# Delta-rule layer: the triangular inverse's small products spread behind projection products, its two 64-row blocks side by side

## The chip, the cores and the metric

The kernel runs on one core of a Trainium2 chip (trn2). The metric is the device time of one execution in microseconds (us), the median of several runs. In the text PE is TensorE (matrix products; PEld its weight loads), DVE is VectorE, ACT is ScalarE, POOL is GpSimd and SP is SyncE, which issues the DMAs here.

## The reference

The kernel computes one inference step of a two-layer decoder trunk for a prompt of 1024 tokens and 64 sample tokens (8 sequences of 8). Layer 0 mixes by a gated delta rule, layer 1 by dilated window attention. The change touches layer 0 alone. There each of 8 heads projects keys, queries and values, runs them through a causal convolution of width 4, and then, in chunks of tokens, solves a unit lower triangular system whose matrix comes from the keys:

```python
proj = jnp.einsum('bld,de->ble', h, w_in)
qkv, new_buf = causal_conv_silu(qkv, conv_buf, conv_w)
kb = kc * bc[..., None]
n_mat = jnp.where(strict, jnp.einsum('nbhik,nbhjk->nbhij', kb, kc) * decay, 0.0)
a_mat = n_mat + jnp.eye(C, dtype=n_mat.dtype)
rhs = jnp.concatenate([vc * bc[..., None], kb * jnp.exp(gc)[..., None]], axis=-1)
sol = lax.linalg.triangular_solve(a_mat, rhs, left_side=True, lower=True, unit_diagonal=True)
...
S, o = lax.scan(step, S0, (w_val, k_cum, qk, q_dec, k_dec, g_tot))
```

The scan then carries the state S from chunk to chunk. The reference uses chunks of 64 tokens; the kernel takes 128 tokens a chunk, 8 chunks of the prompt (the sample tokens are a ninth part with a path of their own), and forms the inverse of the triangular matrix of each chunk explicitly.

## The kernel before

Everything of layer 0 is done head by head, in stages that are emitted one after the other. `stage_k(h)` makes the keys: `conv_tile` loads a 1024x128 weight tile, splits it into a high and a low part, and `project` (line 128) runs 72 products for three column blocks of 384, 384 and 320 tokens (8 slices of the contraction by 3 combinations of high and low parts, 24 products a block), each into a bank called pp. These are the projection products. Each block then passes through the convolution on ACT, DVE and GpSimd (tiles xin and ca, line 72). After that come transposes (line 600), the products of keys with keys (line 655, into ps), the system matrix MT, and small products for the sample tokens (lines 664 to 691).

The inverse of a 128x128 triangular matrix is built up from its diagonal blocks of 32 rows. The 32x32 blocks of MT go to DRAM and back (line 696 writes msc, line 699 reads Mi), so that all 32 blocks of a head lie one on a partition, four times over; a substitution chain of 62 instructions on DVE (lines 710 and 712: a product into vtmp, a sum into Vi, once per row) inverts them; line 714 writes the result vsc and line 719 reads it into Vt, now as diagonal blocks of 8 matrices of 128x128. `stage_qv(h)` makes queries and values in the same way as the keys.

`stage_inverse(h)` completes Vt. Line 766 transposes the eight matrices (eight products 128x128, copied by ACT at line 767 into VT). Then, for the two 64-row blocks one after the other (p0 of 0 and 64): eight products 32x32 of MT and VT (line 773), an ACT copy into Aw (line 774), eight products 32x32 of Aw and Vt (line 777), and a DVE copy into Vt (line 778). The last step joins the two 64-row halves: eight transposes 64x64 (line 782) and a copy (783), eight products 64x64 (line 786) and a copy (787), eight products (line 790) and the DVE copy of line 791. Then `keys_by_token` uses Vt (lines 809 and 810), and DVE turns the result into vn (line 812). All these products write banks of one pool called lv, which has two buffers (`sbank`).

`stage_scan(h)` is the chain over the chunks: products at lines 896, 899, 907 and 910 (bank sc), with DVE steps between them (line 72, tiles w, S and o), `finish` (lines 828 to 835: a norm, a transpose at 832, a copy, a store), and between the hops the small products of the sample tokens, `sample()` (lines 850, 861, 867 and 877).

The emission order is keys 0, queries and values 0, keys 1, inverse 0; then for each head h: scan h, queries and values h+1, keys h+2, inverse h+1; the output gate's products stand with heads 6 and 7. The engines run their own instructions strictly in order. This order isn't the emitted one: a scheduler of the framework, with its own estimate of durations, sorts each engine's instructions, and `order_after` adds an edge that only orders two instructions of one engine. `newest[0]` holds the last product of the latest projection block.

Instructions on fp32 operands show as two passes in the trace (a count of x16 for eight products); the order listing counts products once.

## Time and profile before

| | |
|---|---|
| median of three runs | 2446.84 us (2445.88 to 2450.79) |
| the profiled execution | 2428.75 us, of which its span is 2427.0 us |
| PE busy | 2282.0 us, 94% of the span |
| DVE busy | 1376.6 us, 57% |
| ACT busy | 941.6 us, 39% |
| POOL busy | 260.4 us, 11% |
| chain that ended last | PE 67%, DMA 13%, DVE 9%, issue 6% |

The profiled execution is one run; its span is the time from the first to the last instruction of the trace. Busy time of PE counts a product until its modelled end, so that a busy PE can still be one that runs products slowly. The granted clock is the share of full speed that PE was given in a stretch; 0.50 is half speed.

### The profile page before, as it was taken

How to read it: one execution, taken by the hardware profiler on the slowest of the kernel's cores; microseconds unless marked ns; L12 is line 12 of the kernel's file. 1: busy time of each engine (PE TensorE's matmuls, PEld its weight loads, DVE VectorE, ACT ScalarE, POOL GpSimd, SP SyncE). 2: the span in 40 equal slices, each digit the busy share in tenths (PEclk: the TensorE clock that was granted, in tenths of full speed). 3: DMA queues.
4: the chain of work that ended last, by engine and by line, in shares of the span. 5: the costliest groups of instructions: out<-in, count | busy, mean ns of one | idle time of the engine just before them, and what ended most of it. 6: DMA issues, size and time to landing. Idle time of an engine off the chain costs nothing.

```text
span 2427.0 us, 43290 instructions
## 1 busy us (share of the span) xinstructions
PE 2282.0 (94%) x16647; PEld 2147.1 (88%) x16647; DVE 1376.6 (57%) x3414; ACT 941.6 (39%) x2477; POOL 260.4 (11%) x418
## 2 busy tenths in 40 slices
PE   7799999999999999899999999899998999999997
PEld 5688788779889898799988999899998999999897
DVE  6678767866875437327643374633737337375334
ACT  6445444444544324333233432334323333225234
POOL 3213222222321102200000000000000000000000
PEclk9889889888989999799999999999999999999999
DMA  9223223233223355439732497744967349785634
GB/s 324 62 68 91 63 74 84 60 73 79 79 77 97 88 158 165 131 84 335 228 109 74 132 345 204 237 115 125 351 197 249 115 122 340 198 288 169 213 103 148
DMA packets 482255, 379.42 MB, mean 156 GB/s; under 512 B 46206, under 2 KB 457071, under 8 KB 482048
## 3 DMA queue, kind: packets, MB, share of 16 engines
q1 hardware_dynamic: 482048, 376.65, 51.4%
q8 instruction: 131, 2.15, 0.4%
q14 instruction: 76, 0.62, 0.1%
HBM read 322.31 MB, written 54.27 MB: 155 GB/s over the span
## 4 chain that ended last, share of the span: by engine, by line
PE 67%; DMA 13%; DVE 9%; issue 6%; ACT 3%; POOL 1%; SPq 1%; POOLq 0%; ACTq 0%; DVEq 0%
PE pp L128 46%; DMA DT<-gcscr 2%; PE ps L1182 2%; PE ps L1200 2%; DMA qb<-qscr 2%; PE sc L1400 2%; DVE pr L1351 1%; DMA kc<-in_cache_kv_w_dram 1%; DMA wraw<-in_a_w_in_dram 1%; PE ps L1146 1%; DMA out_kv_s_dram<-knew 1%; PE ps L1191 1%; DMA aw<-in_ada_w_dram 1%; PE ps L150 1%; DMA out_y_p_dram<-yn 1%
## 5 line engine op out<-in xcount | busy, mean ns | idle before, releaser
L128 PE MATMUL pp<-hh,whi 128*128 128x384 f32 (+1 forms) x2688 | 915.2, 341 | 12.2 <-DVE vT L1140 4.2
L128 PE MATMUL pp<-hl,whi 128*128 128x384 f32 (+1 forms) x2688 | 906.1, 337 | 1.3 <-POOL hl L211 1.3
L128 PE MATMUL pp<-hh,wlo 128*128 128x384 f32 (+1 forms) x2688 | 901.5, 336 | 1.2 <-DVE wlo L111 1.2
L128 PEld LDWEIGHTS pp<-hh,whi 128*128 128x128 f32 x2688 | 514.0, 191 | 25.5 <-DVE vT L1140 6.6
L128 PEld LDWEIGHTS pp<-hl,whi 128*128 128x128 f32 x2688 | 514.6, 191 | 9.1 <-issue 4.6
L128 PEld LDWEIGHTS pp<-hh,wlo 128*128 128x128 f32 x2688 | 512.9, 191 | 6.3 <-issue 2.7
L111 DVE TENSOR_TENSOR wlo<-wraw,whi 128x1024 fp32r<-128x1024 f32 x136 | 170.2, 1251 | 127.7 <-ACT whi L110 126.9
L110 ACT CAST whi<-wraw 128x1024 fp32r<-128x1024 f32 x144 | 150.6, 1046 | 235.2 <-PE pp L128 146.2
L1187 ACT ACTIVATE sm<-sm,stg 128x128 f32<-128x128 f32 (+1 forms) x192 | 86.6, 451 | 359.8 <-DVE stg L1185 317.5
L1351 DVE TENSOR_TENSOR pr<-kc,qb 128x1024 f32<-128x1024 f32 x128 | 154.9, 1219 | 89.9 <-DMA qb<-qscr 56.2
L1341 DVE TENSOR_REDUCE ST<-pr 128x8 f32<-128x1024 f32 x128 | 153.7, 1214 | 1.1
L435 POOL TENSOR_TENSOR ol<-zo,oh 128x384 fp32r<-128x384 f32 x9 | 9.2, 1017 | 1302.6 <-ACT oh L434 1285.7
L72 DVE SCALAR_TENSOR_TENSOR ca<-xin,cwT,ca 128x384 f32<-128x384 f32 (+1 forms) x216 | 130.4, 608 | 7.6 <-ACT ca L577 6.2
L1185 DVE CUSTOM_DVE_ANT_0 sm<-ps,mA 128x256 f32<-128x256 f32 (+1 forms) x128 | 48.3, 377 | 137.1 <-PE ps L1182 136.2
L1200 PE MATMUL ps<-vnat,pT 128*128 128x128 f32 x560 | 96.3, 279 | 4.4 <-DVE pT L1196 4.4
L710 DVE TENSOR_TENSOR vtmp<-Vi,Mi 128x2 f32<-128x2 f32 (+30 forms) x248 | 95.7, 386 | 4.4 <-PE ps L690 0.7
L1182 PE MATMUL ps<-kT,qT 128*128 128x128 f32 (+1 forms) x384 | 93.3, 324 | 3.8 <-DVE stg L1185 3.6
L1200 PEld LDWEIGHTS ps<-vnat,pT 128*128 128x128 f32 x560 | 85.6, 189 | 10.6 <-ACT pTn L1380 4.2
L1194 ACT COPY pT<-ps 128x256 f32<-128x256 f32 (+1 forms) x96 | 32.4, 337 | 114.7 <-PE ps L1191 113.5
L128 PE MATMUL pp<-oh,whi 128*128 128x384 f32 (+1 forms) x216 | 72.0, 333 | 2.7 <-DVE zt L72 2.7
L72 DVE SCALAR_TENSOR_TENSOR hh<-pp,GT,xr 128x384 f32<-128x384 f32 (+1 forms) x48 | 27.3, 571 | 83.0 <-PE pp L128 79.2
L1185 DVE CUSTOM_DVE_ANT_0 sm<-ps,mG 128x128 f32<-128x128 f32 x64 | 18.4, 288 | 98.6 <-PE ps L1182 69.1
(449 smaller groups left out, 3681.5 us busy)
## 6 DMA issues: line engine op xcount, KB each, us to landing
qb<-qscr SPq DMA_DIRECT2D x128, 512.0 KB
kc<-in_cache_kv_w_dram SPq DMA_DIRECT2D x104, 512.0 KB
vc<-in_cache_kv_w_dram SPq DMA_DIRECT2D x104, 512.0 KB
wraw<-in_b_w_in_dram SPq DMA_DIRECT2D x80, 512.0 KB
wraw<-in_a_w_in_dram SPq DMA_DIRECT2D x32, 512.0 KB
wraw<-in_ada_w_dram SPq DMA_DIRECT2D x24, 512.0 KB
stgc<-gscr SPq DMA_DIRECT2D x32, 260.0 KB
aw<-in_ada_w_dram SPq DMA_DIRECT2D x8, 1024.0 KB
```

The costliest lines, as they stand in the source:

```text
L72: return (eng or V).scalar_tensor_tensor(out=out, in0=in0, scalar=scalar, in1=in1, op0=op0, op1=op1)
L110: A.copy(out=hi, in_=raw)
L111: (eng or V).tensor_tensor(out=lo, in0=raw, in1=hi.bitcast(F32), op=ALU.subtract)
L128: mm = PE.matmul(acc[:, :cn], lhsT=a[:, k, :], rhs=b[k][:, c0:c0 + cn], start=(n == 0), stop=(n == 3 * KD - 1))
L710: V.tensor_tensor(out=tv, in0=Vi[:, :na, :w], in1=Mi[:, :w, c].unsqueeze(1).broadcast_to([P, na, w]), op=ALU.mult)
L1182: PE.matmul(sv, lhsT=qT[:, b * P:(b + 1) * P], rhs=kT[:, k0:k0 + w], start=True, stop=True)
L1185: V.tensor_tensor_reduce(out=sm[:, :w], in0=sv, in1=mk, scale=1.0, scalar=3e38, op0=ALU.add, op1=ALU.min, accum_out=stg[:, b, 128:129])
L1187: A.activation(out=sm[:, :w], in_=sm[:, :w], func=AF.Exp, scale=-1.0, bias=stg[:, b, 128:129], accum_out=stg[:, b, 129:130])
L1200: PE.matmul(ob[:, (b % 4) * P:(b % 4 + 1) * P], lhsT=pT[:, i * P:(i + 1) * P], rhs=vnat[:, k0 // P + i, :], start=(i == 0), stop=(i == w / ...
L1341: V.tensor_reduce(out=sv[:, n:n + 4, :], in_=pr.rearrange("p (n a e) -> p n a e", a=2, e=P), op=ALU.add, axis=AX.X)
L1351: V.tensor_tensor(out=out, in0=k, in1=q, op=ALU.mult)
L1400: mm = PE.matmul(od[32 * j:32 * j + 8, f * P:(f + 1) * P], lhsT=Z[g][:, a * NB + 2 * j + c, 8 * k:8 * k + 8], rhs=vc[:, j, a * P:(a + 1) * P],
```

## The change

The part of `stage_inverse` that completes Vt becomes a generator, `inverse_steps`. `weave(h)` makes it, and `project` steps it once behind each projection product; each small product gets an order edge behind the newest projection product, which is now noted after every product. `weave(0)` stands ahead of keys 1, and `weave(h + 1)` ahead of queries and values h+1, so that the small products of a head are emitted along with the next projection tile or two. Between two groups of products that wait for a copy, the generator pauses for 8 projection products. The two 64-row blocks are no longer one after the other: the two banks of the first products are filled in alternation, then copied, then the two banks of the second products. What isn't emitted by the time `stage_inverse` is reached is emitted there. The products, the copies and their sizes are the same.

```diff
@@ -116,7 +116,8 @@
                           mybir.DependencyInfo(mybir.DependencyClass.NoSync, mybir.DependencyReason.SCHED_ONLY),
                           reason=reason)
 
-    newest = [None]
+
+    newest, woven = [None], []
 
     def project(w, hh, hl, cb, chunks=CHUNKS, each=None):
         whi, wlo = w
@@ -130,7 +131,9 @@
                     if each:
                         each(mm)
                     n += 1
-            newest[0] = mm
+                    newest[0] = mm
+                    if woven:
+                        next(woven[0], None)
             cb(ci, acc)
 
     def ada_load(layer, ct, pool, ahead):
@@ -756,39 +759,72 @@
             V.tensor_tensor(out=vn[:m, cs, :], in0=v3(bk[b][:m, :n]), in1=bc(sk[:m, cs], P), op=ALU.mult)
         head.update(qT=qT, rq=rq, erq=erq, erqs=erqs, kqs=kqs, vn=vn)
 
-    def stage_inverse(h, head):
-        kT, kN, bp, MT, Vt, vn = (head[n] for n in ("kT", "kN", "bp", "MT", "Vt", "vn"))
-
+    def weave(h):
+
+        woven[:] = [inverse_steps(heads[h])] if h < NH else []
+
+    def inverse_steps(head):
+
+        MT, Vt = head["MT"], head["Vt"]
+
+        def put(mm):
+            order_after(mm, newest[0], "between the products of a projection")
+
+        def pause(n):
+            for _ in range(n):
+                yield
         VT = sb.tile([P, 8, P], F32, name="VT", tag="b4", bufs=1)
         for b in range(2):
             tb = sbank()
             for q in range(4):
-                PE.transpose(tb[:, q * P:(q + 1) * P], Vt[:, b * 4 + q, :], ident)
+                put(PE.transpose(tb[:, q * P:(q + 1) * P], Vt[:, b * 4 + q, :], ident))
+                yield
             A.copy(out=VT[:, b * 4:b * 4 + 4, :], in_=v3(tb))
         Aw = sb.tile([P, 8, 64], F32, name="Aw", tag="Aw")
-        for p0 in (0, 64):
-            pr, qr = slice(p0, p0 + 32), slice(p0 + 32, p0 + 64)
-            ab_ = sbank()
-            for c in range(8):
-                PE.matmul(ab_[qr, c * 32:(c + 1) * 32], lhsT=MT[pr, c, qr], rhs=VT[pr, c, pr], start=True, stop=True)
-            A.copy(out=Aw[qr, :, 0:32], in_=ab_[qr, 0:256].rearrange("p (c n) -> p c n", n=32))
-            vb = sbank()
-            for c in range(8):
-                PE.matmul(vb[pr, c * 32:(c + 1) * 32], lhsT=Aw[qr, c, 0:32], rhs=Vt[qr, c, qr], start=True, stop=True)
-            V.tensor_copy(out=Vt[pr, :, qr], in_=vb[pr, 0:256].rearrange("p (c n) -> p c n", n=32))
+        yield from pause(8)
+        pq = [(slice(p0, p0 + 32), slice(p0 + 32, p0 + 64)) for p0 in (0, 64)]
+
+        ab_ = [sbank() for _ in pq]
+        for c in range(8):
+            for (pr, qr), a in zip(pq, ab_):
+                put(PE.matmul(a[qr, c * 32:(c + 1) * 32], lhsT=MT[pr, c, qr], rhs=VT[pr, c, pr], start=True, stop=True))
+            yield
+        for (pr, qr), a in zip(pq, ab_):
+            A.copy(out=Aw[qr, :, 0:32], in_=a[qr, 0:256].rearrange("p (c n) -> p c n", n=32))
+        yield from pause(8)
+        vb = [sbank() for _ in pq]
+        for c in range(8):
+            for (pr, qr), a in zip(pq, vb):
+                put(PE.matmul(a[pr, c * 32:(c + 1) * 32], lhsT=Aw[qr, c, 0:32], rhs=Vt[qr, c, qr], start=True, stop=True))
+            yield
+        for (pr, qr), a in zip(pq, vb):
+            V.tensor_copy(out=Vt[pr, :, qr], in_=a[pr, 0:256].rearrange("p (c n) -> p c n", n=32))
+        yield from pause(8)
         lo, up = slice(0, 64), slice(64, 128)
         tb = sbank()
         for c in range(8):
-            PE.transpose(tb[:64, c * 64:(c + 1) * 64], Vt[lo, c, lo], ident[:64, :64])
+            put(PE.transpose(tb[:64, c * 64:(c + 1) * 64], Vt[lo, c, lo], ident[:64, :64]))
+            if c % 2:
+                yield
         A.copy(out=VT[lo, :, lo], in_=tb[:64, :].rearrange("p (c n) -> p c n", n=64))
+        yield from pause(8)
         ab_ = sbank()
         for c in range(8):
-            PE.matmul(ab_[up, c * 64:(c + 1) * 64], lhsT=MT[lo, c, up], rhs=VT[lo, c, lo], start=True, stop=True)
+            put(PE.matmul(ab_[up, c * 64:(c + 1) * 64], lhsT=MT[lo, c, up], rhs=VT[lo, c, lo], start=True, stop=True))
+            yield
         A.copy(out=Aw[up], in_=ab_[up, :].rearrange("p (c n) -> p c n", n=64))
+        yield from pause(8)
         vb = sbank()
         for c in range(8):
-            PE.matmul(vb[lo, c * 64:(c + 1) * 64], lhsT=Aw[up, c, :], rhs=Vt[up, c, up], start=True, stop=True)
+            put(PE.matmul(vb[lo, c * 64:(c + 1) * 64], lhsT=Aw[up, c, :], rhs=Vt[up, c, up], start=True, stop=True))
+            yield
         V.tensor_copy(out=Vt[lo, :, up], in_=vb[lo, :].rearrange("p (c n) -> p c n", n=64))
+
+    def stage_inverse(h, head):
+        kT, kN, bp, Vt, vn = (head[n] for n in ("kT", "kN", "bp", "Vt", "vn"))
+        while woven:
+            for _ in woven.pop():
+                pass
 
 
         kds = sb.tile([NS, P], F32, name="kds", bufs=1)
@@ -942,10 +978,12 @@
 
     stage(stage_k, 0)
     stage(stage_qv, 0)
+    weave(0)
     stage(stage_k, 1)
     stage(stage_inverse, 0)
     for h in range(NH):
         stage(stage_scan, h)
+        weave(h + 1)
         stage(stage_qv, h + 1)
         stage(stage_k, h + 2)
         stage(stage_inverse, h + 1)
```

The scheduler decides where these products come to stand. First, PE in the middle of layer 0, at the inverse of head 3. In the kernel before it begins behind the last projection product of the keys of head 4 (MT_3926 and Vt_4095 are head 3's, Aw is the copied product, S and DT_2860 belong to the scan of head 2):

```order
L128 MATMUL pp<-hh_754,wlo 128x384
L664 MATMUL ps<-tri_s,gall 64x64
L773 MATMUL lv<-VT,MT_3926 32x32 x4
L907 MATMUL sc<-S,qT_3391 128x128
L773 MATMUL lv<-VT,MT_3926 32x32 x4
L667 MATMUL ps<-kT_4806 64x64
L910 MATMUL sc<-w,DT_2860 128x128
L777 MATMUL lv<-Vt_4095,Aw 32x32 x7
L832 MATMUL sc<-ident,o 128x128
L777 MATMUL lv<-Vt_4095,Aw 32x32
L773 MATMUL lv<-VT,MT_3926 32x32 x7
```

In the changed kernel the same part (now lines 790 and 798, MT_4010 and Vt_4179) reads:

```order
L658 MATMUL ps<-kT_4890 128x128
L946 MATMUL sc<-w,DT_2944 128x128
L658 MATMUL ps<-kT_4890 128x128 x7
L129 MATMUL pp<-hl_658,whi 128x320
L129 MATMUL pp<-hh_657,wlo 128x320
L798 MATMUL lv<-Vt_4179,Aw 32x32 x2
L943 MATMUL sc<-S,qT_3391 128x128
L798 MATMUL lv<-Vt_4179,Aw 32x32 x14
L129 MATMUL pp<-hh_731,whi 128x320
L129 MATMUL pp<-hl_732,whi 128x320
L129 MATMUL pp<-hh_731,wlo 128x320
L129 MATMUL pp<-hh_761,whi 128x320
```

There each group of 16 products of the two blocks is one run, with the keys' projection products ahead of it and behind it; 26 more of that projection's products follow behind the rows shown, where none followed before.

Second, PE at the inverse of head 1, where it also begins at the end of the next keys' projection. Before (MT_1799, Vt_1968):

```order
L773 MATMUL lv<-VT,MT_1799 32x32 x4
L907 MATMUL sc<-S,qT_1265 128x128
L773 MATMUL lv<-VT,MT_1799 32x32 x4
L832 MATMUL sc<-ident,o 128x128
L667 MATMUL ps<-kT_2678 64x64
L910 MATMUL sc<-w,DT_1088 128x128
L777 MATMUL lv<-Vt_1968,Aw 32x32 x8
L773 MATMUL lv<-VT,MT_1799 32x32 x8
L896 MATMUL sc<-S,kT_854 128x128
L677 MATMUL ps<-ident,Us 64x64
L777 MATMUL lv<-Vt_1968,Aw 32x32 x8
L782 MATMUL lv<-ident,Vt_1968 64x64 x8
```

After (MT_1873, Vt_2042):

```order
L790 MATMUL lv<-VT,MT_1873 32x32 x5
L667 MATMUL ps<-tri_s,gall 64x64
L129 MATMUL pp<-hh_754,whi 128x384
L129 MATMUL pp<-hl_755,whi 128x384
L129 MATMUL pp<-hh_754,wlo 128x384
L868 MATMUL sc<-ident,o 128x128
L946 MATMUL sc<-w,DT_1088 128x128
L670 MATMUL ps<-kT_2762 64x64
L798 MATMUL lv<-Vt_2042,Aw 32x32 x16
L932 MATMUL sc<-S,kT_854 128x128
L680 MATMUL ps<-ident,Us 64x64
L806 MATMUL lv<-ident,Vt_2042 64x64 x8
```

There the four runs of eight have become two of sixteen, the first of them partly ahead of the last three projection products; the rest stands where it stood.

Third, DVE behind the inverse of head 3, where the substitution chain of head 4 (the rows that write vtmp with 128x2, 128x3 and so on) begins. Before:

```order
L72 SCALAR_TENSOR_TENSOR w<-sc,bp,vn_3737 128x128
L791 COPY Vt_4095<-lv 64x8x64
L72 SCALAR_TENSOR_TENSOR o<-sc,rq,t_4393 128x128
L710 TENSOR_TENSOR vtmp<-Vi,Mi 128x2
L72 SCALAR_TENSOR_TENSOR S<-S,egt,sc 128x128
L712 TENSOR_REDUCE Vi<-vtmp 128x1
L710 TENSOR_TENSOR vtmp<-Vi,Mi 128x3
L712 TENSOR_REDUCE Vi<-vtmp 128x1
L710 TENSOR_TENSOR vtmp<-Vi,Mi 128x4
L712 TENSOR_REDUCE Vi<-vtmp 128x1
```

After (the last copy of the inverse is now line 821, vn is line 848, the chain is lines 713 and 715):

```order
L821 COPY Vt_4179<-lv 64x8x64
L72 SCALAR_TENSOR_TENSOR w<-sc,bp,vn_3821 128x128
L848 TENSOR_TENSOR vn_4886<-lv,bp 128x512
L72 SCALAR_TENSOR_TENSOR S<-S,egt,sc 128x128
L690 TENSOR_TENSOR su<-ps,ident 64x64
L72 SCALAR_TENSOR_TENSOR o<-sc,rq,t_4393 128x128
L865 TENSOR_SCALAR so<-so 128x1
L848 TENSOR_TENSOR vn_4886<-lv,bp 128x512
L867 TENSOR_SCALAR o<-o,so 128x128
L166 TENSOR_SCALAR SC_98<-ps,vecs 128x9
L72 SCALAR_TENSOR_TENSOR o<-sc,rq,t_4417 128x128
L713 TENSOR_TENSOR vtmp<-Vi,Mi 128x2
```

The chain's first row stood two rows behind the last copy of the inverse and ahead of the first product that makes vn; it now stands behind both of those.

## Rows read from the trace of the kernel before

**Rows 1.** The page: busy us (share of the span) and instructions of PE.

```profile
PE 2282.0 (94%) x16647; PEld 2147.1 (88%) x16647; DVE 1376.6 (57%) x3414; ACT 941.6 (39%) x2477; POOL 260.4 (11%) x418
```

**Rows 2.** The page: shares by engine of the chain that ended last.

```profile
PE 67%; DMA 13%; DVE 9%; issue 6%; ACT 3%; POOL 1%; SPq 1%; POOLq 0%; ACTq 0%; DVEq 0%
```

**Rows 3.** Windows: the third of six stretches, and their sum: busy us, PEclk, DMA share, GB/s.

```profile
412.80:446.80 34.00, 31.32 (x251) 24.48 (x251) 20.50 (x66) 14.94 (x47) 10.24 (x16) 0.69 0.23 62
...
sum 183.20, PE 166.66 PEld 134.04 DVE 111.54 ACT 85.12 POOL 54.01; mean PE 27.78 PEld 22.34 DVE 18.59 ACT 14.19 POOL 9.00
```

**Rows 4.** Windows of 7 us, columns as before: two inside the third stretch, one among projections.

```profile
419.00:426.00 7.00, 7.00 (x54) 5.56 (x55) 1.44 (x6) 1.96 (x6) 0.00 (x0) 0.50 0.32 85
...
426.00:433.00 7.00, 6.48 (x32) 5.72 (x30) 5.31 (x15) 3.54 (x11) 2.74 (x2) 0.52 0.01 3
...
461.00:468.00 7.00, 7.00 (x49) 6.93 (x49) 7.00 (x23) 4.11 (x16) 2.84 (x5) 1.00 0.33 89
```

**Rows 5.** Timeline of PE, heads 3 and 4: start us, us, line, op, out<-in, passes.

```profile
415.61 0.21 PE L773 MATMUL lv<-VT,MT 32*32 32x32 f32 x1
...
417.92 0.63 PE L782 MATMUL lv<-ident,Vt 64*64 64x64 f32 x8
...
420.65 1.97 PE L786 MATMUL lv<-VT,MT 64*64 64x64 f32 x16
...
504.43 0.21 PE L773 MATMUL lv<-VT,MT 32*32 32x32 f32 x1
...
506.26 0.63 PE L782 MATMUL lv<-ident,Vt 64*64 64x64 f32 x8
```

**Rows 6.** Timeline of ACT: the copy of the second round in head 3.

```profile
416.67 0.36 ACT L774 COPY Aw<-lv 32x256 f32<-32x256 f32 x1
```

**Rows 7.** Timelines of PE, DVE and SP: one round from chain to chain.

```profile
403.57 3.42 SPq L719 DMA_DIRECT2D Vt<-vsc  x4
...
408.63 1.95 PE L655 MATMUL ps<-kT 128*128 128x128 f32 x16
...
410.42 0.82 PE L766 MATMUL lv<-ident,Vt 128*128 128x128 f32 x6
...
428.02 0.16 DVE L710 TENSOR_TENSOR vtmp<-Vi,Mi 128x2 f32<-128x2 f32 x1
...
492.29 1.84 SPq L719 DMA_DIRECT2D Vt<-vsc  x4
...
499.41 0.82 PE L766 MATMUL lv<-ident,Vt 128*128 128x128 f32 x6
...
515.83 2.35 DVE L710 TENSOR_TENSOR vtmp<-Vi,Mi 128x2 f32<-128x2 f32 x1
```

**Rows 8.** Timeline of PE, head 0's inverse, which lies among projection products.

```profile
177.09 0.31 PE L128 MATMUL pp<-hh,wlo 128*128 128x320 f32 x1
...
177.33 0.24 PE L777 MATMUL lv<-Vt,Aw 32*32 32x32 f32 x2
...
178.02 0.21 PE L773 MATMUL lv<-VT,MT 32*32 32x32 f32 x1
...
178.05 0.19 PE L777 MATMUL lv<-Vt,Aw 32*32 32x32 f32 x1
...
181.99 1.03 PE L786 MATMUL lv<-VT,MT 64*64 64x64 f32 x15
```

**Rows 9.** Timeline of PE: a product of the scan, with what it waited for.

```profile
439.19 0.33 PE L832 MATMUL sc<-ident,o 128*128 128x128 f32 x1 [1.48 <-DVE o L831]
```

**Rows 10.** Chain of waits by time: start us, us, projection products in a row.

```profile
401.24 0.88 PE pp L128 x6
...
484.79 4.19 PE pp L128 x24
```

**Rows 11.** Timeline of DVE: the second product that makes vn, head 3.

```profile
434.44 0.69 DVE L812 TENSOR_TENSOR vn<-lv,bp 128x512 f32<-128x512 f32 x1 [0.33 <-PE lv L810]
```

## The prediction

> **What bounds the kernel now.** I read the busy times first: TensorE (PE) is busy for 2282.0 us, 94% of the span [rows 1]. The chain of work that ended last is PE for 67% and VectorE (DVE) for 9% [rows 2]. So PE's own order sets the time, and a change counts as far as it takes idle or slow time out of PE. Next I read where PE is slow. For each of heads 1 to 6 there is one stretch, some 24 to 34 us long, in which no projection product (the pp products of `project`, line 128) stands: the inverse of that head, the scan of the head before it and the sample's small products fill it alone. The windows of these six stretches sum to 183.2 us with PE busy for 166.6 us, so it idles for 16.6 us, and the third (head 3's) has a mean granted clock of 0.69 [rows 3]. Among projection products the clock is 1.00, as at 461 to 468; inside the third stretch it stands at 0.50 to 0.52 for 14 us on end [rows 4]. The timeline of that stretch shows the two 32-row rounds of the inverse one after the other, each a chain of PE, an ACT copy, PE and a DVE copy [rows 5, 6].
>
> A second loop runs on DVE, once a head: the substitution chain on Vi (lines 710 and 712) starts at 428.02, just behind the copy that ends an inverse; the DMAs that bring its result back to Vt are issued until 494.13 (492.29 + 1.84); the transposes on Vt start at 499.41, and the next chain starts at 515.83, again just behind the inverse [rows 7]. That loop is 87.8 us, the same as PE's round of a head. Both are tight, so a gain on PE lasts only if this loop shrinks too; it holds the inverse itself (499.41 to 515.83, 16 of its 88 us), which is what the change shortens.
>
> **The change part by part.** Nothing is added or dropped: the products and copies are the same in number and size.
>
> *Two blocks side by side.* In head 3 the second round runs from the first L773 product of the block that follows L777 at 415.61 to the transposes L782 at 417.92, 2.3 us; in head 4 it is 504.43 to 506.26, 1.8 us, and the other heads of the stretches lie between these [rows 5]. With both blocks at once the round goes, but the second block's ACT copy (0.36 us) now stands ahead of the joint L777 run [rows 6]: net 1.5 us on a round of 1.8 to 1.9. Where the two blocks' products already meet at 178.02, one line's starts at 178.02 and the other's at 178.05, where one line alone steps by 0.03 us (16 in a run of 0.5 us) [rows 8]; whether a joint run is shorter than two, it lies inside the 1.5. Where the inverse stays in its stretch, as the order shows for heads 1 and 2 and nearly for 4 and 5, I take the 1.5 us in full: 4 x 1.5 = 6.0 us. The page "TensorEngine Tiling (Array Packing)" of the Trainium skill, section "Key Properties", has different tiles execute in parallel, which the two lines at 178.02 and 178.05 neither bear out nor exclude; it also says that changing the tiling mode drains the array, which speaks against laying 32x32 products between projection products. The next term is what the row shows of that, whatever its cause.
>
> *Products moved out of the stretch.* PE's order has 800 calls in the six stretches before and 650 after: 134, 135, 135, 135, 127, 134 become 117, 117, 89, 109, 122, 96. In heads 3 and 6 the whole 32x32 part moves up among projection products, in head 4 most of sample()'s products move down among them. A call in a stretch costs 183.2 / 800 = 0.23 us; among projection products it costs its own step, from 0.03 us (32x32) to 0.21 us (128x128), some 0.10 on the mean. So 150 x 0.13 = 19 us is the most this can bring. At the least it brings nothing: the stretch also ends with the scan's last hops, one of whose products waits 1.48 us for DVE at 439.19 whatever stands ahead of it [rows 9]. Between 0 and 19 I take the middle, 9.5 us, since only half of a stretch (the part up to the copy L791) is the inverse.
>
> *Switching.* Around a small run PE loses a little: the L128 product at 177.09 is followed by L777 at 177.33, 0.24 us later, where a projection product's step is 0.15 (0.88 / 6) [rows 8, 10]. That is 0.1 us, and I take as much for the way back: 0.2 us for each run, some 7 runs in each of heads 3 and 6, 2.8 us lost.
>
> *Copies, pauses, queues.* ACT and DVE get the same copies, two at a time; at some 0.36 us each [rows 6] they lie beside PE. The scheduling edges add no wait on the chip; they only move order. GpSimd's work isn't moved on purpose, and SyncE's order changes from head 3 on because the DMAs of Vi and Vt follow DVE. Heads 0 and 7 have their inverse among projection products already: nothing, bounded by 1.9 us each either way. Layer 1's order barely changes: nothing.
>
> Sum: -6.0 - 9.5 + 2.8 = -12.7 us. Against the profiled execution (2428.75, of which 1.75 lies outside the span) that is 2416.0; the median of the runs is 18.1 us higher, and on its scale the forecast is 2446.8 - 12.7 = 2434 us. Parts from 0 to 19 and the switching give 2425 to 2444.
>
> **The rivals.**
>
> *Nothing is gained, the DVE loop holds (2442 to 2451).* DVE is full, 7.00 of 7 us, at 461 to 468 [rows 4]. If the substitution chain and its DMAs (66.1 us from 428.02 to 494.13) are the longer loop, the inverse merely waits later. For it: PE's transposes start only 5.3 us behind the last Vt issue [rows 7]. Against it: the loop contains the inverse, which gets shorter.
>
> *Slower: early transposes wait for Vt.* PE runs in order. In head 3 (and much the same in 6) the Vt transposes now stand ahead of 48 projection products, 24 at 0.147 (0.88 / 6) and 24 at 0.175 us (4.19 / 24) [rows 10], and of the 16 L655 passes (1.95 us [rows 7]): 3.5 + 4.2 + 1.95 = 9.6 us earlier in PE's order. The Vt issues end at 406.99 (403.57 + 3.42), and PE reaches L766 at 410.42: at most 3.4 us of slack [rows 7]. If Vt is no earlier than now, PE stands for 9.6 - 3.4 = 6.2 us a head. And in head 4's round DVE's order puts the next substitution chain behind the second vn product, which in the trace ends at 435.13 (434.44 + 0.69) and not at 428.02: 7.1 us later [rows 7, 11], so that its Vt is late as well. Against it: head 3's chain ends some 12 convolution steps earlier in DVE's order. Two stands and the late chain make 19.5 us; it decides from 12.7 us on, that is from two stands. If the delay passes on to heads 4 to 7 as well, 4 x 6.2 + 7.1 = 32 us. So +7 to +19: 2454 to 2466, and the likely one is 2456.
>
> *More: the clock holds.* A 64x64 run of 16 takes 1.97 us at half clock (420.65) and 1.03 us for 15 at full clock (181.99) [rows 5, 8]; the clock fell to 0.50 at 419 after PE had done small products alone since 412.8. With projection products between them, or with a shorter stretch, it may not fall: head 3's 14 us at half clock would shrink by up to 7 us, and six such by 42. I count half of the heads: another 20 us, 2414. The page "TensorE: Matmul & The Clock Gate" of the Trainium skill (section "The HAM clock gate") has the same two levels, 1.2 and 2.4 GHz, and lets PE's activity decide between them; the fall at 419 agrees. For heads 1 and 2 the order leaves the second half of the stretch as it was, which speaks against the full 42.
>
> *It doesn't do what it says.* The pace "one small product behind each projection product" is only a lower bound in the order: in heads 1 and 2 the small products still come in runs of 11, 5 and 16 with no projection products between. If heads 3 to 6 gain nothing from it, only the 6.0 us of the round are left: 2441.
>
> **How the numbers follow.** Forecast (2425 to 2442) 0.40; clock 0.15 (2404 to 2425); nothing gained 0.17; not what it says 0.08; slower 0.20. What a measurement of this kernel can tell from no change is about 0.2%, 4.9 us, so faster means below 2442. Faster: 0.40 + 0.15 + 0.03 of the last case but one = 0.58; slower 0.21 with a little of the case where nothing is gained; the rest, 0.21, is the same. The range takes in most of the clock case and the lighter half of the slower one: 2412 to 2456.
>
> **What would show it.** Right: the six stretches without projection products shrink from 183.2 us to some 165 in all, the third most (34.0 to about 28), one L773-like run of 16 and one L777-like run of 16 per head where four stood, and the period from chain to chain on DVE falls from 87.8 to about 86. Wrong by waiting: PE idle ahead of the Vt transposes of heads 3 and 6, released by a DMA. Wrong by DVE: the same period of 88 us with more idle PE. Clock: a mean granted clock in the stretches above 0.8. The forecast fails if the time that leaves the stretches turns up as idle PE ahead of the scan's hops or of the convolution tiles.

## The result and the profile after

The changed kernel runs in 2411.78 us (median of four runs, 2411.01 to 2423.21) where the kernel before takes 2446.36 (four runs). The ratio is 0.9873, with a 95% interval of 0.9834 to 0.9911: 31 us faster, 22 to 41. The profiled execution of the changed kernel took 2412.29 us with a span of 2410.6.

The page of the changed kernel, PE's busy time and the shares of the chain that ended last (for [rows 1, 2]):

```profile
PE 2250.9 (93%) x16647; PEld 2116.5 (88%) x16647; DVE 1375.5 (57%) x3414; ACT 937.6 (39%) x2477; POOL 257.6 (11%) x418
...
PE 65%; DMA 11%; DVE 11%; issue 7%; ACT 3%; POOL 1%; SPq 1%; POOLq 0%; ACTq 0%; DVEq 0%
```

The instructions are the same in number (16647 products), and PE is busy for 31 us less (2282.0 before). Products that are the same and take less busy time point to the clock: over the whole span PE stands at half clock for 245 us before and for 185 us after, 60 us less, and half of that is 30.

The six stretches without projection products, cut as for [rows 3] (window, busy time of PE, PEld, DVE, ACT, POOL, then PEclk, DMA share, GB/s):

```profile
238.40:265.00 26.60, 21.71 (x215) 16.84 (x214) 19.27 (x62) 13.70 (x42) 9.68 (x15) 0.87 0.27 75
321.50:351.40 29.90, 23.89 (x215) 17.75 (x213) 21.09 (x68) 13.21 (x42) 9.60 (x15) 0.81 0.25 68
413.10:437.60 24.50, 20.73 (x169) 14.96 (x167) 15.26 (x47) 12.52 (x44) 9.28 (x14) 0.82 0.24 67
494.80:514.10 19.30, 17.28 (x200) 15.24 (x199) 11.63 (x39) 12.22 (x37) 6.76 (x13) 0.91 0.36 95
572.80:597.30 24.50, 19.92 (x218) 17.28 (x217) 15.71 (x58) 13.70 (x42) 6.50 (x13) 0.93 0.33 87
660.20:682.40 22.20, 19.23 (x174) 14.16 (x173) 14.52 (x45) 12.95 (x45) 6.91 (x13) 0.90 0.26 68
sum 147.00, PE 122.76 PEld 96.23 DVE 97.49 ACT 78.31 POOL 48.73; mean PE 20.46 PEld 16.04 DVE 16.25 ACT 13.05 POOL 8.12
```

They sum to 147.0 us, 36 us less than the 183.2 of before, and the granted clock in the third is 0.82 where it was 0.69. I cut each stretch into the inverse part (to the last copy of the inverse), the keys part (to the last product of `keys_by_token`) and the tail (to the first projection product). The inverse parts alone, first of the kernel before, heads 1, 4 and the sum of six:

```profile
237.00:250.40 13.40, 13.40 (x150) 11.12 (x149) 3.86 (x13) 5.17 (x17) 1.48 (x4) 0.67 0.36 94
...
502.00:514.50 12.50, 12.50 (x151) 10.57 (x152) 4.44 (x16) 4.86 (x15) 1.99 (x5) 0.73 0.41 104
...
sum 78.10, PE 78.10 PEld 64.38 DVE 26.12 ACT 31.61 POOL 10.93; mean PE 13.02 PEld 10.73 DVE 4.35 ACT 5.27 POOL 1.82
```

and of the changed kernel:

```profile
238.40:246.10 7.70, 7.70 (x118) 6.45 (x116) 3.74 (x13) 4.37 (x15) 1.56 (x4) 1.00 0.42 113
...
494.80:505.10 10.30, 10.30 (x155) 8.45 (x154) 4.56 (x17) 5.52 (x19) 2.02 (x5) 1.00 0.48 121
...
sum 47.80, PE 46.38 PEld 38.05 DVE 20.80 ACT 25.03 POOL 9.03; mean PE 7.73 PEld 6.34 DVE 3.47 ACT 4.17 POOL 1.51
```

78.1 us have become 47.8, and the clock there is 1.00 in all six heads where it was 0.67 to 0.76. In heads 3 and 6 part of this is products that left the stretch; in head 4, whose order kept everything behind the transposes in it, 12.5 us have become 10.3 by clock and rounds. The timeline of PE in head 1 shows the joint runs (for [rows 5]; start us, us, line, operation, passes):

```profile
238.96 1.09 PE L798 MATMUL lv<-Vt,Aw 32*32 32x32 f32 x32
...
240.49 0.61 PE L806 MATMUL lv<-ident,Vt 64*64 64x64 f32 x8
...
241.92 0.97 PE L813 MATMUL lv<-VT,MT 64*64 64x64 f32 x13
...
244.32 1.03 PE L819 MATMUL lv<-Vt,Aw 64*64 64x64 f32 x15
```

One run of 32 passes (16 products) takes 1.09 us. The 64x64 runs take 0.97 us for 13 passes (L813) and 1.03 for 15 (L819), where [rows 5] has 1.97 for 16 at half clock: this is full clock.

The rest moves less: the keys part takes 48.6 us before and 44.5 after, the tail 56.5 and 54.7, and the projection blocks around the stretches 8 us more in all (683.4, 675.5 before), most of it where heads 3 and 6 do products of the inverse in them. The result is 36.2 - 8 = 28 us over layer 0 (848.4 us, 876.2 before). The rest of the execution, layer 1, takes from 1430 to 1445 us in the profiled executions and was short in the one of before (1429.6; 1439.0 in the one after), so that the two lie only 16.5 us apart; layer 0 is the better measure, and the experiments are compared there. Its lengths come from one execution each, and the ratios from all of them: e2_weave below is 10.6 us shorter than before in layer 0, yet its ratio is 0.9983.

### The profile page after: what moved, and what is told of

It reads as the page before. It is cut to its first block, busy times and chain, and to the rows that moved or that the text cites. A ratio compares the mean times of both kernels' runs of the same rounds, so it can differ in the third digit from the quotient of the medians.

```text
span 2410.6 us, 43253 instructions
## 1 busy us (share of the span) xinstructions
PE 2250.9 (93%) x16647; PEld 2116.5 (88%) x16647; DVE 1375.5 (57%) x3414; ACT 937.6 (39%) x2477; POOL 257.6 (11%) x418
## 4 chain that ended last, share of the span: by engine, by line
PE 65%; DMA 11%; DVE 11%; issue 7%; ACT 3%; POOL 1%; SPq 1%; POOLq 0%; ACTq 0%; DVEq 0%
PE pp L129 47%; PE ps L1238 2%; PE ps L1220 2%; DMA DT<-gcscr 2%; PE sc L1438 2%; DMA wraw<-in_a_w_in_dram 2%; DVE vtmp L713 2%; DMA qb<-qscr 1%; PE ps L1184 1%; DVE pr L1389 1%; PE ps L1229 1%; DVE ca L72 1%; DMA oscr<-stgc 1%; PE ps L153 1%; DMA out_y_p_dram<-yn 1%
## 5 line engine op out<-in xcount | busy, mean ns | idle before, releaser
L110 ACT CAST whi<-wraw 128x1024 fp32r<-128x1024 f32 x144 | 150.7, 1046 | 230.0 <-PE pp L129 148.2
L72 DVE SCALAR_TENSOR_TENSOR hh<-pp,GT,xr 128x384 f32<-128x384 f32 (+1 forms) x48 | 27.4, 571 | 82.4 <-PE pp L129 78.7
L129 PE MATMUL pp<-oh,wlo 128*128 128x384 f32 (+1 forms) x216 | 71.9, 334 | 1.5 <-DVE wlo L111 1.5
```

The lines of the kernel that those rows point to most:

```text
L72: return (eng or V).scalar_tensor_tensor(out=out, in0=in0, scalar=scalar, in1=in1, op0=op0, op1=op1)
L110: A.copy(out=hi, in_=raw)
L129: mm = PE.matmul(acc[:, :cn], lhsT=a[:, k, :], rhs=b[k][:, c0:c0 + cn], start=(n == 0), stop=(n == 3 * KD - 1))
```

## The experiments

Layer 0 is here the time from the first projection product behind the early stretch at 100 us to the first one behind the stretch at its end. Two readings explain its length in every kernel: the time in which PE is idle, and the time for which its clock stands at half. The next table has both, with the ratio to the kernel before (the ratio over all executions of a kernel, the rest from the profiled one). "Half" sums the profile's record of the granted clock; the last column is PE's busy time less half of that, so what the work would take at full clock.

| kernel | ratio to before (95%) | layer 0, us | PE idle | half clock | busy - half/2 |
|---|---|---|---|---|---|
| before | 1 | 876.2 | 52.7 | 166.2 | 740.4 |
| t_swap: one after the other, lower first | 0.9941 (0.9923 to 0.9958) | 868.2 | 48.0 | 154.8 | 742.8 |
| e2_weave: early emission alone | 0.9983 (0.9960 to 1.0005) | 865.6 | 51.0 | 142.0 | 743.6 |
| e11_weave_swap: the same, lower first | 0.9898 (0.9850 to 0.9946) | 859.6 | 51.1 | 136.0 | 740.5 |
| e1_side: side by side alone | 0.9836 (0.9805 to 0.9868) | 841.4 | 44.8 | 121.2 | 736.0 |
| e8_inturn: the same, not alternating | 0.9847 (0.9828 to 0.9867) | 841.4 | 46.0 | 104.1 | 743.3 |
| e9_side_swap: side by side, lower first | 0.9876 (0.9826 to 0.9927) | 850.6 | 51.2 | 113.4 | 742.8 |
| the change | 0.9873 (0.9834 to 0.9911) | 848.4 | 63.0 | 83.8 | 743.5 |
| e6_noedge: the change without edges | 0.9871 (0.9841 to 0.9902) | 849.1 | 62.2 | 87.9 | 742.9 |
| e10_after_swap: the change, lower first | 0.9820 (0.9776 to 0.9864) | 838.2 | 49.6 | 90.7 | 743.3 |
| x_before_late: before, sample products late | 0.9910 (0.9886 to 0.9934) | 858.7 | 38.8 | 131.7 | 754.1 |
| x_side_late: e1_side, sample products late | 0.9940 (0.9913 to 0.9967) | 867.2 | 47.7 | 129.9 | 754.5 |
| x_after_late: the change, sample products late | 0.9992 (0.9968 to 1.0015) | 877.7 | 63.3 | 150.7 | 739.1 |

The windows over layer 0 that the table rests on, for the kernel before, e1_side and the changed kernel (PE busy first, PEclk third from the end):

```profile
121.20:997.40 876.20, 823.49 (x5912) 741.67 (x5912) 597.39 (x1692) 390.54 (x1159) 210.46 (x327) 0.91 0.34 92
```

```profile
122.20:963.60 841.40, 796.60 (x5912) 720.77 (x5912) 590.01 (x1692) 389.72 (x1159) 217.92 (x327) 0.93 0.35 96
```

```profile
123.20:971.60 848.40, 785.38 (x5911) 705.59 (x5912) 595.89 (x1693) 387.59 (x1160) 208.01 (x327) 0.95 0.35 95
```

Busy and idle time make up the length by definition; what is found is that the last column stays within 736 to 744 us for the ten kernels that leave the sample products in their place, while half-clock time runs from 84 to 166. So, within those 8 us, the length follows idle time and half clock. From before to the change, half-clock time falls by 82.4 us, worth 41.2, idle time rises by 10.3 and the last column by 3.1: 41.2 - 10.3 - 3.1 = 27.8 us.

The price of half clock shows with the order held still too. Of the 39 executions of the kernel before that the experiments were timed against, the five with the highest mean granted clock (0.948 on the mean) took 2437 us, the five with the lowest (0.939) 2457: by these clocks some 47 us more at half clock go with 20 us more time. The profiled execution of before (0.95) lies at the favourable end of them, so the table is likelier to understate a gain than to overstate it.

**Side by side alone (e1_side).** In the kernel before, `stage_inverse` gets the two rounds, without the generator:

```diff
-        for p0 in (0, 64):
-            pr, qr = slice(p0, p0 + 32), slice(p0 + 32, p0 + 64)
-            ab_ = sbank()
+        pq = [(slice(p0, p0 + 32), slice(p0 + 32, p0 + 64)) for p0 in (0, 64)]
+        ab_ = [sbank() for _ in pq]
             for c in range(8):
+            for (pr, qr), a in zip(pq, ab_):
...
```

> The kernel before with one edit: in stage_inverse the two 64-row blocks are side by side (two runs of 16 small products for four of 8), emitted where they were, without the generator. If the round that goes carries the gain: 6 to 8 heads x 1.5 us, so 9 to 12 us less than before (ratio 0.995 to 0.996), and half-clock time little changed. If the place of emission carries it, by way of the granted clock: PE's order still has 778 calls in the six stretches without projection products (800 before, 650 in the changed kernel), so half-clock time between 160 and 800 us stays near 130 us and the ratio is 0.996 to 1.002.

It ran in 2406.3 us, ratio 0.9836: this part alone brings as much as the change, and neither expectation said so. Nor does this kernel's gain lie where the rounds are. The inverse parts, heads 1, 3 and the sum:

```profile
236.60:247.80 11.20, 11.20 (x147) 9.27 (x147) 3.63 (x13) 5.36 (x18) 1.44 (x4) 0.76 0.43 111
...
404.50:417.40 12.90, 12.02 (x166) 9.85 (x166) 6.02 (x27) 7.08 (x22) 2.11 (x6) 1.00 0.44 109
...
sum 81.30, PE 80.42 PEld 65.55 DVE 29.73 ACT 35.93 POOL 12.70; mean PE 13.40 PEld 10.92 DVE 4.95 ACT 5.99 POOL 2.12
```

81.3 us, not less than the 78.1 of before; half-clock time there is 43 us (45 before). What shrank is the tail. The tails of the kernel before, heads 1, 3 and the sum, and then those of e1_side:

```profile
258.40:269.10 10.70, 8.11 (x61) 5.17 (x60) 9.47 (x29) 5.24 (x16) 5.35 (x9) 0.83 0.08 23
...
435.30:446.80 11.50, 9.37 (x60) 6.06 (x60) 9.36 (x29) 5.32 (x17) 5.35 (x9) 0.68 0.08 23
...
sum 56.50, PE 43.74 PEld 28.80 DVE 48.09 ACT 27.24 POOL 27.77; mean PE 7.29 PEld 4.80 DVE 8.01 ACT 4.54 POOL 4.63
```

```profile
255.80:264.90 9.10, 7.20 (x61) 4.14 (x60) 7.96 (x29) 5.42 (x20) 7.28 (x10) 0.89 0.44 105
...
424.10:427.00 2.90, 2.90 (x45) 2.26 (x44) 2.83 (x12) 2.66 (x9) 2.30 (x7) 1.00 0.02 4
...
sum 20.90, PE 18.29 PEld 13.15 DVE 19.58 ACT 15.92 POOL 17.20; mean PE 3.05 PEld 2.19 DVE 3.26 ACT 2.65 POOL 2.87
```

56.5 us became 20.9: most of sample()'s last products (lines 861, 867 and 877 before) stand among projection products now. Nothing in the edit asks for that; the scheduler's order came out so. Of the 45 us of half clock that are gone, 22 were in the tails and 16 outside the stretches.

**Early emission alone (e2_weave).** In the changed kernel the two blocks go one after the other again:

```diff
-        ab_ = [sbank() for _ in pq]
-        for c in range(8):
-            for (pr, qr), a in zip(pq, ab_):
...
+        for p0 in (0, 64):
+            pr, qr = slice(p0, p0 + 32), slice(p0 + 32, p0 + 64)
+            ab_ = sbank()
+            for c in range(8):
...
```

> The changed kernel with one edit: the two 64-row blocks one after the other again (four rounds), emitted behind the projection products as in the changed kernel. PE's order has 766 calls in the stretches. If the place of emission alone carries the gain: ratio 0.987 to 0.990. If both parts are needed to take products out of the stretches: only about a quarter of the calls that the changed kernel takes out are out here (34 of 150), so a quarter of 34 us, 8 us, ratio 0.996 to 0.998.

0.9983, no difference that can be told. In the profiled execution its half-clock time is 24 us lower all the same. The second expectation was nearly right (0.996 to 0.998); but the second order of the same idea (e11_weave_swap, below) says how far one order can be trusted.

**Without the edges (e6_noedge).** `put` does nothing:

```diff
         def put(mm):
-            order_after(mm, newest[0], "between the products of a projection")
+            pass
```

> The changed kernel without its order edges: each small product may stand anywhere. The order of all five engines comes out the same as the changed kernel's, instruction for instruction. If the pace behind the projection products did anything on the chip, the ratio would rise towards 1; if the edges are idle, the ratio is that of the changed kernel, 0.987 within 0.004, and the profile shows the same stretches (149 us in all against 185 before) within 5 us.

0.9871, the change's ratio, and the six stretches sum to 146.1 us (147.0 in the change; the expectation's 149 and 185 count the last projection product in). The instruction order of all five engines is that of the changed kernel, and in this second execution of the same order the clock of the inverse parts is again 1.00 in all six heads. So the edges do nothing; what is left of the first half of the change is that the inverse is emitted earlier, along with the next projections. What the pauses of 8 do was not measured.

**Added products (e4_filled).** In the kernel before, behind every second small product, one product whose result nothing reads (28 a head):

```diff
             for c in range(8):
                 PE.matmul(ab_[qr, c * 32:(c + 1) * 32], lhsT=MT[pr, c, qr], rhs=VT[pr, c, pr], start=True, stop=True)
+                if c % 2:
+                    PE.matmul(ab_[:, 256:512], lhsT=hh[0][:, 0:P], rhs=hh[0][:, 0:256], start=True, stop=True)
...
```

> The kernel before with added products that nothing reads: behind every second small product of the inverse one more on operands that are there already (256 columns in fp32r in the 32-row rounds, 64 columns in fp32 in the 64-row ones), 28 a head, into unused columns or partitions of the same banks; some 0.11 us each at full clock, 3 us a head, 25 us in all. If the half clock is what costs in the stretches and comes of PE doing small products alone: half-clock time between 160 and 800 us falls from 130 to below 90 us, the mean clock in the stretches rises above 0.8, and the time pays back most of the added work: 2440 to 2455 us. If waits between the small products set the time and the clock only follows: the clock stays near 0.72 and the time is 2446 plus 10 to 25 us, 2456 to 2471.

2544.84 us, ratio 1.040 (1.037 to 1.043). It was to hold the clock and did the contrary: half-clock time in layer 0 rose from 166 to 257 us. The timeline of PE shows why it can't serve as a test:

```profile
253.01 0.31 PE L773 MATMUL lv<-VT,MT 32*32 32x32 f32 x4
253.24 0.38 PE L775 MATMUL lv<-hh 128*128 128x256 f32 x1
253.56 0.31 PE L773 MATMUL lv<-VT,MT 32*32 32x32 f32 x4
253.79 0.39 PE L775 MATMUL lv<-hh 128*128 128x256 f32 x1
```

Four 32x32 passes and one 128x128 product of 256 columns take 0.55 us (253.01 to 253.56) where their own steps are about 0.13 (four of 0.032) and, as an estimate, 0.12 (two thirds of a 384-column product's 0.175): 0.3 us for two changes of form, at full clock. The 128 such pairs of the 32-row rounds would make 38 us at full clock, and at half clock a pair takes 0.86 us. So this run can't say what the clock alone is worth; for that there are the table and the 39 executions of one order.

**Products block by block (e8_inturn).** e1_side with the loops exchanged, 8 products of one block and then 8 of the other:

```diff
-        for c in range(8):
-            for (pr, qr), a in zip(pq, ab_):
+        for (pr, qr), a in zip(pq, ab_):
+            for c in range(8):
...
```

> The kernel with the two blocks side by side alone, and their products block by block (8 and 8) and not in alternation: the same two rounds, the same copies. If what the array does with alternating blocks counts: 32 passes saved at 16 ns in two runs, 1 us a head, 8 us slower than with alternation (ratio 0.987). If only the number of rounds counts: the same as with alternation, 0.984 within 0.004. If the scheduler's order of everything else decides (732 calls in the stretches, 778 with alternation): anywhere between 0.980 and 1.000, with a tail that has nothing to do with the inverse.

0.9847 against 0.9836: alternating the blocks brings nothing that can be measured, and two rounds for four keep the gain. Its order differs from e1_side's in every engine, yet layer 0 has the same length, 841.4 us.

**A null edit (t_swap).** In the kernel before, the lower block first:

```diff
-        for p0 in (0, 64):
+        for p0 in (64, 0):
```

> The kernel before with one edit that saves nothing: of the two 64-row blocks the lower comes first. Rounds, products, copies and pools are the same. If gains of this size come from the rounds: ratio 0.998 to 1.002. If the scheduler's rearrangement of everything around the inverse is worth as much as the change (its order has 745 calls in the stretches, 800 before): ratio below 0.995 or above 1.005, with tails or inverse parts that differ from before by 10 us and more.

0.9941, clear of 1: an edit that saves nothing brings 0.6%. Its inverse parts take 88.7 us (10.6 more than before), its tails 27.2 (29 less) and the projection blocks 14 more. So a fresh order alone can be worth half a per cent.

**Second orders (e9_side_swap, e10_after_swap, e11_weave_swap).** The lower block first in e1_side, in the change and in e2_weave:

```diff
-        pq = [(slice(p0, p0 + 32), slice(p0 + 32, p0 + 64)) for p0 in (0, 64)]
+        pq = [(slice(p0, p0 + 32), slice(p0 + 32, p0 + 64)) for p0 in (64, 0)]
```

> The kernel with the two blocks side by side alone, lower block first in each alternation: work and rounds as with the upper first, but the scheduler's order differs (731 calls in the stretches, 778). If the joint rounds bring the gain whatever the order makes of the rest: ratio within 0.006 of 0.984. If it was one lucky order: ratio above 0.990. In both cases the length of layer 0 should be 742 us of PE work plus its idle time plus half of the time at half clock, within 8 us.

> The changed kernel with the lower block first in each alternation (710 calls in the stretches, 650). If the joint rounds bring the gain: ratio within 0.006 of 0.987. If the order that the changed kernel happened to get brings it (inverse parts without half clock): half-clock time in the inverse parts rises above 20 us and the ratio goes above 0.992.

> The changed kernel with the two blocks one after the other again, the lower one first: a second order for the early emission alone (798 calls in the stretches, 766 with the upper first, which had the ratio 0.998). If early emission alone is worth nothing: 0.990 to 1.002. If the 0.998 was an unlucky order and the emission is worth as much as the joint rounds: below 0.990.

0.9876, 0.9820 and 0.9898: the first two as expected for joint rounds, the third at the border of its two cases. Side by side has now five orders, with ratios of 0.982 to 0.988; one after the other has four, 0.990 to 1. The two groups don't overlap, though the intervals of the nearest two do. Their means are 0.985 and 0.9955, so the joint rounds are worth about 1.0% on the mean of the orders, and orders of one idea lie 0.4 to 0.9% apart. Early emission: 1 and 0.994 become 0.998 and 0.990 (0.3%) with separate rounds, with joint ones the mean is 0.985 in either case; that is too small to tell from the scatter. With the lower block first the change took 2405.11 us, and e1_side 2406.3: both are nominally faster than the change, by less than the intervals.

The means over the orders of the table, without e6_noedge, tell the two halves of the change apart:

| | half clock, us | PE idle, us |
|---|---|---|
| one after the other, emitted late (2 orders) | 160.5 | 50.4 |
| one after the other, emitted early (2) | 139.0 | 51.1 |
| side by side, emitted late (3) | 112.9 | 47.3 |
| side by side, emitted early (2) | 87.2 | 56.3 |

Joint rounds go with some 50 us less at half clock, early emission with some 24 us less, worth 12; with joint rounds 9 us more idle time take most of that back.

**Sample products late (x_before_late, x_after_late, x_side_late).** As the tails gave e1_side its gain, sample()'s products are emitted behind the next head's queries and values, in the kernel before, in the change and in e1_side:

```diff
             S = Sn
-            next(steps, None)
...
-        for _ in steps:
-            pass
+        head.update(steps=steps)
...
         stage(stage_qv, h + 1)
+        for _ in heads[h].pop("steps"):
+            pass
```

> The kernel before with one edit: the sample tokens' small products (sample(), four groups) are emitted after the queries and values of the next head and not between the hops of the scan, so that they may stand among projection products; the inverse is as before. PE's order has 603 calls in the six stretches (800 before). If the tail of a stretch (from the last product of keys_by_token to the first projection product, 56 us in six heads before, 21 us with the blocks side by side alone) is what can be had: tail below 25 us and the ratio 0.984 to 0.990. If the inverse's half clock is what counts: half-clock time in the inverse parts stays near 45 us and the ratio is 0.996 to 1.004.

> The changed kernel with the same edit (544 calls in the stretches, 650 in the changed kernel). If the two gains are of different time (the inverse part at full clock, the tail without the last scan hops and sample products), they add: layer 0 ends 25 to 35 us earlier than the changed kernel's 972 us, 2378 to 2390 us, ratio 0.972 to 0.977. If they are one and the same time: 2400 to 2416 us, ratio 0.982 to 0.988.

> Blocks side by side alone, and the sample tokens' small products emitted after the queries and values of the next head (614 calls in the stretches). If both gains add (0.984 and 0.991): 0.975 to 0.980, 2386 to 2398 us, the fastest. If the late products take back what the joint rounds bring, as they did with the changed kernel: 0.988 to 1.000, with idle or half-clock time in layer 0 above that of the side-by-side kernel (44.8 and 121.2 us).

0.9910, 0.9992 and 0.9940; the first two lie outside both cases of their expectations, the third is the case that takes the gain back. The tails go as wanted (in all six heads of x_before_late a projection product stands ahead of the last product of `keys_by_token`), but its projection blocks take some 41 us more (717, 675.5 before), the inverse parts run at half clock for 56 of their 97 us, and the work at full clock grows to 754 us in two of the three. The gains don't add: time pushed out of one part turned up in another. No version came out of this that clearly beats the change.

## Why the prediction was right in its direction and small in its size

*What bounds the kernel.* Right: PE's own order, and within it idle and slow time. The table's last column shows it better than the chain did. The six stretches shrank to 147.0 us and the third to 24.5, more than the 165 and 28 that were to show it right. What the sum did wrong was to leave the clock as it was: time at half clock stands in none of its terms, only in a rival.

*Two blocks side by side, 6.0 us.* This is the term that was mis-sized. Its mechanism (a round less, a copy later) is there, but the five orders with joint rounds are 1.0% faster on the mean than the four without, about 25 us, four times the term. I priced the round at its own place, at an unchanged clock; the runs show that its own place need not get shorter (81 us of inverse parts in e1_side and e8_inturn, 78.1 before) and that the gain appears as half-clock time that is gone (166 us before, 84 to 121 with joint rounds, 136 to 166 without) and as a few microseconds less of idle time in e1_side, e8_inturn and e10_after_swap. Why two joint rounds leave less time at half clock, much of it away from the rounds, is not shown.

*Products moved out of the stretch, 9.5 us.* Neither borne out nor refuted with separate rounds (0.3%, some 7 us, less than the scatter of the orders); with joint rounds it can't be told from nothing. Where the products moved (heads 3 and 6), the stretches shrank but the projection blocks ahead of them grew by 6 us each. The price of a product outside was read too low as well: 0.03 us is one pass, and a 32x32 product has two (1.09 us for 16).

*Switching, 2.8 us lost.* Right in sign and short in price: I read 0.2 us for the way in and out, e4_filled shows 0.3. The change agrees in head 3: eight 32x32 passes between two projection products put 0.60 us between the starts of these (398.953 to 399.553), of which 0.15 is a projection step and 0.25 are the eight passes, and the next projection step is 0.25 and not 0.15, so 0.3 us in all. The page "TensorEngine Tiling (Array Packing)" of the Trainium skill, section "Key Properties", has a change of the tiling mode drain the array. The rows agree with a price for each change, 0.15 us at full clock in e4_filled; whether it is the draining or a weight load that no longer hides behind the product before, they don't tell.

*The rival on the clock* is what happened, by its time and its sign, and I gave it 0.15. It forecast 2414 us (2404 to 2425) and a mean clock in the stretches above 0.8; the median is 2411.8 and the clocks are 0.81 to 0.93. Its reason, projection products between the small ones, holds for the smaller part: early emission goes with a third of the half-clock time that left, joint rounds with two thirds. It was held back by reading that the order of heads 1 and 2 hardly changes, and that the clock there would therefore fall as before. It doesn't: in the kernel before it fell 4.5 to 6.2 us into each of the six stretches, within the inverse; in the changed kernel it held for 15.5 to 19.7 us in all six and fell behind the inverse, in the keys part or the tail. The fall at 419 in the kernel before came with PE counted busy without a gap (6.20 of 6.20 us from 412.8 on), so that PE's busy time alone doesn't tell when the clock holds. The range (2412 to 2456) ends just at the measured time: the median lies 0.2 us below it, and the ratio times the time before, 2446.84 x 0.9873 = 2416, lies in it. That the range reaches so far is owed to this rival; the sum's own 2434 is 22 us off.

*The rival on the Vt wait* didn't come. All waits of the transposes for a DMA in the changed kernel are 1.0 us in two cases:

```profile
  DMA Vt<-vsc: 1.0, 2
```

The substitution chain of head 4 did start behind the second vn product, as the order said, 7.4 us behind the copy (417.04 to 424.42), which is the 7.1 us of the forecast; yet PE hardly waited for it:

```profile
416.36 0.68 DVE L821 COPY Vt<-lv 64x512 f32<-64x512 f32 x1 [0.87 <-PE ps L685]
...
423.03 0.69 DVE L848 TENSOR_TENSOR vn<-lv,bp 128x512 f32<-128x512 f32 x1 [0.72 <-PE lv L846]
...
424.42 0.34 DVE L713 TENSOR_TENSOR vtmp<-Vi,Mi 128x2 f32<-128x2 f32 x1
```

The round that ends with this late start took 91.4 us (89.8 before), the next one, to 505.25, 80.8 (87.8 in [rows 7]); over the five rounds from head 2's chain to head 7's the mean is 84.7 us, 86.7 before. So the loop on DVE took a start 7 us late without making PE wait and shrank with PE; it isn't the bound, and *nothing gained* fell with it.

*It doesn't do what it says* came true in part: the edges behind the projection products change nothing in any head (e6_noedge), and the order is the scheduler's.

## What to carry to other kernels

Where a scheduler sets the order, an edit redraws the order of everything around it: run a null edit and a second order of the same idea before believing a few tenths of a per cent, and look for the gain in the whole layer, not at the edited lines. Cut a tensor-bound stretch into busy time at full clock, half of the half-clock time, and idle time; here that sum held within 8 us over ten kernels and showed where the time went, though not why the clock fell. Joining two short dependent rounds into one paid more than its own latency.

## What the runs showed of the hardware that was not expected

Small products of different form cost more in changing between them than in running: 0.55 us for a pair whose own steps are an estimated 0.25 us, so that a PE that is busy without a gap (253.0 to 254.9 in e4_filled) does less than half of what it could.

The granted clock of the same small products in nearly the same order (heads 1 and 2) was 0.67 and 0.72 in the inverse parts before and 1.00 after; e1_side, with joint rounds as well, held it only in head 3 (1.00) and fell in the others, 3.4 to 6.0 us into the stretch. In head 1 the runs come closest to the reason. In the three kernels with joint rounds and late emission (e1_side, e8_inturn, e9_side_swap) the clock fell 5.1 to 5.9 us into that stretch; in the three with joint rounds and early emission (the change, e6_noedge, e10_after_swap) it held for 19.5 to 22.0. PE does nearly the same runs there; what differs next to the stretch is that the first joint run stands behind the last projection product in e1_side and ahead of the last three in the change:

```profile
236.29 0.34 PE L128 MATMUL pp<-hh,wlo 128*128 128x384 f32 x1
236.56 0.43 PE L773 MATMUL lv<-VT,MT 32*32 32x32 f32 x8
...
237.34 0.69 PE L773 MATMUL lv<-VT,MT 32*32 32x32 f32 x24
```

```profile
236.09 0.65 PE L790 MATMUL lv<-VT,MT 32*32 32x32 f32 x22
...
237.09 0.37 PE L790 MATMUL lv<-VT,MT 32*32 32x32 f32 x10
...
238.10 0.34 PE L129 MATMUL pp<-hh,wlo 128*128 128x384 f32 x1
```

So where some 1.1 us of 32x32 runs stand, ahead of three large products or behind them, goes with whether the clock falls within the inverse; in the change it falls later in this head too, in the tail. Joint rounds aren't needed for it in head 1: with separate rounds and early emission the clock of its inverse part was 1.00 too (e2_weave, e11_weave_swap). What it is about those products stays open: e4_filled, which was to show it, changed too much else.
